# Seven-product output matmuls: in their last chunk every quarter of the output is summed in PSUM and reaches the residual once

## The chip, the core and the metric

The kernel runs on one core of a Trainium2 chip. TensorE (PE) multiplies matrices into PSUM; VectorE (DVE), ScalarE (ACT) and GpSimd (POOL) do everything elementwise; SyncE (SP) starts the DMAs. Each engine runs its own queue in order and meets the others through semaphores. The metric is the time of one execution on the device in microseconds (us), lower is better.

## The reference, cut to what matters

One decoder layer on a sequence of 1024 tokens, width 1024, in float32. Three times the running sum `h` gets a product added to it, scaled by a vector `gt`:

```
h = h + 0.5 * gt1 * (silu(a) * b) @ ffn1_w_out          # inner size 2816: stage i = 0, "FFN1"
h = h + gt2 * (mixed @ w_out)                           # inner size 1024: stage i = 1, "project_out"
h = h + 0.5 * gt3 * (silu(a) * b) @ ffn2_w_out          # inner size 2816: stage i = 2, "FFN2"
return rmsnorm(h, final_norm_w)
```

The change touches these three products and nothing else in the sources.

## The kernel before

`hT` holds `h` transposed in SBUF: eight tiles of 128 features by 1024 tokens. The output of one of the three products is seen as a 2x2 matrix of quarters, each 512 features by 512 tokens, so four tiles (`d` = 0 to 3) of 128x512. `out_seven` computes the 2x2 block product with seven block products instead of eight (the Winograd form of Strassen's scheme). The products are called `q` = 1 to 7, and with P1 to P7 for them the quarters are

```
quarter (0,0): P1 + P2                 quarter (0,1): P1 + P6 + P5 + P3
quarter (1,0): P1 + P6 + P7 + P4       quarter (1,1): P1 + P6 + P7 + P5
```

The inner dimension is cut into pairs of 128 rows; a stage runs over chunks of pairs: `CHUNKS` = (4, 3, 4) in FFN1 and FFN2, and a single chunk (4,) in project_out. Within a chunk the seven products follow each other, and a product of a chunk of 4 has four steps `k`. For a step `ops` forms the two operands (sums and differences of blocks, named s1..s4 on the weight side and t1..t4 on the other, by `left` and `right`, which are GpSimd or VectorE), and splits both into a high and a low part in a tile `wp`: two ScalarE casts (line 677) and two VectorE subtractions (line 678). A step then has 12 matmuls (line 750): four tiles `d` times three (high by high, high by low, low by high). There are four `wp` buffers here, so casts can run at most four steps, one product, ahead of the matmuls. The four 128x512 results of a product stand in PSUM, alternately in a pool named `po` and one named `s`.

`post` takes each result away. In chunks before the last, P1, P5, P6 and P7 are copied by ScalarE to SBUF accumulators `acc` (1, 5, 6, 7), from which the next chunk's PSUM tiles are seeded (line 745: a ScalarE copy into PSUM, after which the matmuls add on top); P2, P4 and P3 go straight into `hT` by `residual` (line 782: one VectorE instruction, `h + gt * x`). In the last chunk the order is 1, 5, 7, 6, 2, 4, 3. There P1, P7 and P6 are copied out and combined in `acc` by GpSimd additions (lines 715 to 727), and parts of the sums go to `hT` as they become known: P1 by one residual (from PSUM), the running sum of P1, P6 (of earlier chunks) and P7 by another (from `acc`, after line 718), P6 of the last chunk by another (from PSUM), the sums for quarters (1,1) and (0,1) by two more (from `acc`, in `second`), and P2, P4, P3 by one each (from PSUM). That is 8 residuals for each `d`, 32 in a stage. project_out has no earlier chunk, so it has no line 715, and its accumulators are parts of the large tiles `u0l` and `u0h`.

Ahead of project_out stands a merge (lines 1220 to 1234), which forms its input `mix`: per tile two DMAs from `d_gab`, matmuls into `po` (line 281), a VectorE multiplication (line 1233) and a GpSimd addition (line 1234). The squares for the norm after a stage (lines 194 to 198: ScalarE, then GpSimd or VectorE additions into `sqacc`) start in its last two products. A scheduler puts the instructions of each engine in order ahead of time, so the order of the code is not the order of the queues.

Of the kernel before, what the change touches and what calls it, by code (L numbers as in the profile page):

```python
# [9 lines left out]
F32 = mybir.dt.float32  # L10
# [7 lines left out]
P = 128  # L18
# [4 lines left out]
H2 = 512  # L23
# [29 lines left out]
class Layer:  # L53
# [541 lines left out]
    def out_seven(self, i, chunks, wsrc, gsrc, free, acc, state, then, have=None):  # L595
# [3 lines left out]
        nc = self.nc  # L599
        o, prs = 0, []  # L600
# [3 lines left out]
        chunks = prs  # L604
# [45 lines left out]
        def ops(c, k, q):  # L650
# [4 lines left out]
            left = nc.vector if len(chunks) == 1 and q in (7, 2) else nc.gpsimd  # L655
# [25 lines left out]
            if q in (2, 6) and (c, k, 8 - q) in done:  # L681
                right.tensor_sub(g("b21"), g("b21"), g("t2"))
                ren("b21", "t4")
                left.tensor_sub(g("a2"), g("a2"), g("s2"))
# [12 lines left out]

        def post(q, d, p, c, last):
            A = {x: acc[x][d] for x in acc}
            if q in (2, 3, 4):  # L700
                res(q == 4, q == 3, d, p, last)
                return
            if q == 6 and last:
                res(1, 0, d, p)
                nc.scalar.copy(A[1], p)
                return
            if q == 1 and last:
                res(0, 0, d, p)
            nc.scalar.copy(A[q], p)
            if not last:  # L710
                return
            w = A[6 if 6 in A else 1]
            if q == 1:
                if 6 in A:
                    nc.gpsimd.tensor_add(w, w, A[1])
            elif q == 7:
                nc.gpsimd.tensor_add(A[5], A[5], w)
                nc.gpsimd.tensor_add(w, w, A[7])
                nc.gpsimd.tensor_add(A[7], A[7], A[5])
                res(1, 0, d, w)  # L720

        def second(d):

            A = {x: acc[x][d] for x in acc}
            nc.gpsimd.tensor_add(A[7], A[7], A[1])
            res(1, 1, d, A[7])
            nc.gpsimd.tensor_add(A[5], A[5], A[1])
            res(0, 1, d, A[5])

        fetch()  # L730
        for c, prs in enumerate(chunks):
            last = c == len(chunks) - 1
            m = len(prs)
            for j, q in enumerate((1, 5, 7, 6, 2, 4, 3) if last else (1, 2, 5, 7, 6, 4, 3)):
                if (len(chunks) - 1 - c + j) % 2 == 0:
                    po = [self.psO.tile([P, H2], F32, name="po") for _ in range(4)]
                else:
                    po = [self.psA.tile([P, 2, H2], F32, name="s") for _ in range(2)]
                    po = [p[:, x, :] for p in po for x in range(2)]


                seeded = c > 0 and q in acc and not (last and q == 6)
                if seeded:
# [848 lines left out]
```

## Time and profile before

| | |
|---|---|
| median of 3 runs | 2452.97 us (2447.19 to 2454.83) |
| the profiled execution | 2450.27 us, its span 2448.5 us |
| busy, of the span | PE 2284.3 us, DVE 1860.7, ACT 1031.7, POOL 1252.7 |
| mean granted clock of TensorE | 0.967 of full speed |
| last chunk of FFN1, its matmuls | 650.14 to 749.85 us |
| last chunk of FFN2, its matmuls | 2329.32 to 2428.65 us |
| project_out, its matmuls | 1624.44 to 1730.8 us |

The span is the time between the first and the last instruction in the trace of one execution; the time of that execution is 1.77 us longer, and it lies 2.7 us below the median. Busy times overlap between engines. A product's four steps have 48 matmuls, and the trace lacks a few of the records.

### The profile page before, as it was taken

To read this page: it belongs to the slowest core of one execution; us is meant where nothing else is said; L and a number is where in the kernel's file an instruction comes from. 1 tells how busy PE (TensorE), PEld (TensorE's weight loads), DVE (VectorE), ACT (ScalarE), POOL (GpSimd) and SP (SyncE) were. 2 spreads that over 40 slices of the span, in tenths; PEclk is the share of its full clock that TensorE was granted. 3 is DMA by queue.
4 is the path that set the end of the run, shared out by engine and by line. 5 is a ranking of instruction groups with operands and counts; after the bars stand their busy time and mean duration, and the time that the engine had idled before them with its cause. 6 is when DMAs were issued, how large, how long until landed. Compare 5 with 4: busy or idle time off the path is not lost.

```text
span 2448.5 us, 32717 instructions
## 1 busy us (share of the span) xinstructions
PE 2284.3 (93%) x11563; PEld 1909.0 (78%) x11563; DVE 1860.7 (76%) x2790; ACT 1031.7 (42%) x1860; POOL 1252.7 (51%) x920
## 2 busy tenths in 40 slices
PE   7799999999977999999989999988889999999997
PEld 5578888878856899888868889866668888887875
DVE  8888887578999856666668887669985555558998
ACT  5333222245744422223348776624432222235655
POOL 3855454444576545555215544456754444435366
PEclk8999999999998999999998999999889999999998
DMA  9135655263204344343551221640322222255201
GB/s 345 56 112 169 201 176 186 86 232 134 78 0 136 97 142 121 110 138 110 167 165 51 74 79 57 213 153 0 103 69 78 82 78 86 85 190 186 94 1 69
DMA packets 248888, 288.32 MB, mean 118 GB/s; under 512 B 14852, under 2 KB 169236, under 8 KB 248724
## 3 DMA queue, kind: packets, MB, share of 16 engines
q1 hardware_dynamic: 248608, 286.19, 36.6%
q8 instruction: 91, 1.49, 0.3%
q14 instruction: 73, 0.60, 0.1%
q10 hardware_dynamic: 116, 0.05, 0.0%
HBM read 216.45 MB, written 69.73 MB: 117 GB/s over the span
## 4 chain that ended last, share of the span: by engine, by line
PE 31%; DVE 12%; DMA 3%; issue 2%; ACT 1%; POOL 1%; SPq 0%; DVEq 0%; ACTq 0%; POOLq 0%
PE po L281 16%; DVE wp L678 4%; PE ot L1166 2%; DVE hT L782 2%; PE po L750 2%; PE pt L1152 2%; PE s L750 2%; PE s L281 2%; PE s L1063 1%; PE s L1064 1%; DMA tn<-d_gab 1%; PE pt L855 1%; PE ot L1163 0%; PE po L495 0%; DMA hT<-d_h 0%
## 5 line engine op out<-in xcount | busy, mean ns | idle before, releaser
L750 PE MATMUL po<-wp 128*128 128x512 f32 x1176 | 293.7, 406 | 30.2 <-DVE wp L678 27.6
L281 PE MATMUL po<-u0h,wp 128*128 128x512 f32 x944 | 305.6, 395 | 9.2 <-DVE gates L991 4.9
L750 PEld LDWEIGHTS po<-wp 128*128 128x128 f32 x1176 | 227.9, 196 | 91.2 <-DVE wp L678 38.1
L281 PE MATMUL po<-u1h,wp 128*128 128x512 f32 x880 | 281.9, 391 | 3.7 <-DVE bias L544 2.2
L750 PE MATMUL s<-wp 128*128 128x512 f32 x1008 | 247.4, 403 | 21.0 <-DVE wp L678 19.7
L750 PEld LDWEIGHTS s<-wp 128*128 128x128 f32 x1008 | 195.9, 195 | 67.3 <-DVE wp L678 24.4
L334 ACT CAST wp<-S 128x1024 fp32r<-128x1024 f32 x98 | 102.9, 1050 | 302.5 <-PE po L281 300.4
L281 PEld LDWEIGHTS po<-u0h,wp 128*128 128x128 f32 x944 | 178.9, 189 | 49.9 <-DVE gates L991 5.1
L463 POOL TENSOR_TENSOR t<-t,t 128x512 f32<-128x512 f32 x38 | 55.3, 1456 | 301.8 <-DVE t L407 191.9
L281 PEld LDWEIGHTS po<-u1h,wp 128*128 128x128 f32 x880 | 165.1, 188 | 40.5 <-DVE bias L544 2.6
L281 PE MATMUL po<-u0l,wp 128*128 128x512 f32 x472 | 185.4, 393 | 0.0
L281 PE MATMUL po<-u1l,wp 128*128 128x512 f32 x440 | 172.5, 392 | 2.6 <-DVE u1l L243 2.6
L335 DVE TENSOR_TENSOR wp<-S,wp 128x1024 fp32r<-128x1024 f32 x98 | 159.8, 1630 | 15.8 <-ACT wp L334 15.6
L334 ACT CAST wp<-raw 128x1024 fp32r<-128x1024 f32 x98 | 82.0, 837 | 186.0 <-PE po L281 174.4
L341 POOL TENSOR_TENSOR S<-raw 128x512 f32<-128x512 f32 x49 | 68.7, 1403 | 157.0 <-DMA raw<-w_in 92.2
L281 PE MATMUL po<-t2h,wp 128*128 128x512 f32 x392 | 132.2, 397 | 2.2 <-ACT t2h L300 2.1
L281 PE MATMUL po<-t3h,wp 128*128 128x512 f32 x392 | 132.1, 398 | 0.2 <-DVE t L395 0.2
L281 PE MATMUL po<-t4h,wp 128*128 128x512 f32 x392 | 131.6, 396 | 0.8 <-DVE tn L399 0.7
L395 DVE TENSOR_TENSOR t<-tn,po 128x512 f32<-128x512 f32 x57 | 39.0, 685 | 110.4 <-issue 78.7
L335 DVE TENSOR_TENSOR wp<-raw,wp 128x1024 fp32r<-128x1024 f32 x98 | 113.6, 1159 | 11.9 <-ACT wp L334 11.8
L1156 DVE TENSOR_TENSOR pl<-pt,ph 128x512 fp32r<-128x512 f32 (+2 forms) x160 | 96.9, 619 | 11.9 <-ACT ph L1155 11.1
L281 PEld LDWEIGHTS po<-u0l,wp 128*128 128x128 f32 x472 | 89.7, 190 | 18.1
(471 smaller groups left out, 6248.4 us busy)
## 6 DMA issues: line engine op xcount, KB each, us to landing
raw<-ffn_w_in SPq DMA_DIRECT2D x88, 512.0 KB, 4.8
raw<-ada_w SPq DMA_DIRECT2D x56, 512.0 KB, 4.4
raw<-w_in SPq DMA_DIRECT2D x40, 512.0 KB, 4.2
d_g<-t SPq DMA_DIRECT2D x50, 256.0 KB, 2.0
d_h<-hT SPq DMA_DIRECT2D x24, 512.0 KB, 5.8
hT<-d_h SPq DMA_DIRECT2D x48, 256.0 KB, 5.3
d_g<-tg SPq DMA_DIRECT2D x38, 256.0 KB, 2.0
fw<-ada_w SPq DMA_DIRECT2D x8, 1024.0 KB, 11.1
```

Of the source, the lines that this page charges most:

```text
L281: nc.tensor.matmul(ps, a, b, start=k == 0 and q == 0, stop=k == n - 1 and q == 2)
L334: nc.scalar.copy(w[:, 0], t)
L335: nc.vector.tensor_sub(w[:, 1], t, f32(w[:, 0]))
L341: nc.gpsimd.tensor_add(s[:, 0:4], b[:, 0:4], b[:, 4:8])
L395: nc.vector.tensor_add(c, u2, p)
L463: nc.gpsimd.tensor_mul(g, g, t)
L678: nc.vector.tensor_sub(w[:, x, 1], g(n[x]), f32(w[:, x, 0]))
L750: nc.tensor.matmul(po[d], l[:, e], r, start=k == 0 and z == 0 and not seeded, stop=k == m - 1 and z == 2, skip_group_check=seeded)
L782: self.nc.vector.scalar_tensor_tensor(h, po, self.ab[:, 3 * i + 2, d:d + 1], h, op0=ALU.mult, op1=ALU.add)
L1152: nc.tensor.transpose(pt[:, o + j * P:o + (j + 1) * P], a, self.ident)
L1156: nc.vector.tensor_sub(lo, pt[:, :n], f32(hi))
L1166: nc.tensor.matmul(ot, self.V2[kt // 4][:, kt % 4, b, g, :], x[:, o:o + 2 * P], start=first and m == 0, stop=last and m == 1)
```

## The change

In the last chunk all seven products get one residual per quarter. In FFN1 and FFN2 every product of the last chunk is now seeded: P1, P5, P6, P7 from their own accumulators, P2 from accumulator 1, P4 from accumulator 7 and P3 from accumulator 6, after GpSimd has added up in them what the quarter needs (`between`). The residuals are then P2 on top of P1 for (0,0), P4 for (1,0), P3 for (0,1), all from PSUM, and one from `acc` for (1,1): 16 in a stage where there were 32. GpSimd has 16 additions of 128x512 for this where there were 24, ScalarE 28 seeds where there were 12, and 16 copies out as before. In project_out the order becomes 1, 5, 7, 2, 6, 4, 3; P1 starts in pool `s` instead of `po`; P4 is accumulated in the same PSUM tiles as P6 (`chain`), P2 and P6 are seeded from accumulator 1 and P3 from accumulator 7: 16 residuals for 32, 16 GpSimd additions for 20, 12 seeds for none, and 16 copies out as before. The number of matmuls, casts and operand sums is the same; one line of operand sums stays on VectorE in project_out as before.

```diff
@@ ops @@
-            left = nc.vector if len(chunks) == 1 and q in (7, 2) else nc.gpsimd
+            left = nc.vector if single and q == 7 else nc.gpsimd
@@
-                left.tensor_sub(g("a2"), g("a2"), g("s2"))
+                (nc.vector if single else left).tensor_sub(g("a2"), g("a2"), g("s2"))
@@ post, second -> post, between @@
-            if q == 6 and last:
-                res(1, 0, d, p)
-                nc.scalar.copy(A[1], p)
-                return
-            if q == 1 and last:
-                res(0, 0, d, p)
-            nc.scalar.copy(A[q], p)
-            if not last:
-                return
-            w = A[6 if 6 in A else 1]
-            if q == 1:
-                if 6 in A:
-                    nc.gpsimd.tensor_add(w, w, A[1])
-            elif q == 7:
-                nc.gpsimd.tensor_add(A[5], A[5], w)
-                nc.gpsimd.tensor_add(w, w, A[7])
-                nc.gpsimd.tensor_add(A[7], A[7], A[5])
-                res(1, 0, d, w)
-
-        def second(d):
-            A = {x: acc[x][d] for x in acc}
-            nc.gpsimd.tensor_add(A[7], A[7], A[1])
-            res(1, 1, d, A[7])
-            nc.gpsimd.tensor_add(A[5], A[5], A[1])
-            res(0, 1, d, A[5])
+            nc.scalar.copy(A[1 if q == 6 and single else q], p)
+            if last and q == 1 and not single:
+                nc.gpsimd.tensor_add(A[6], A[6], A[1])
+
+        def between(q):
+            for d in range(4):
+                A = {x: acc[x][d] for x in acc}
+                if single:
+                    if q == 2:
+                        nc.gpsimd.tensor_add(A[1], A[1], A[7])
+                        nc.gpsimd.tensor_sub(A[7], A[5], A[7])
+                    elif q == 6:
+                        nc.gpsimd.tensor_add(A[5], A[5], A[1])
+                        res(1, 1, d, A[5])
+                        nc.gpsimd.tensor_add(A[7], A[7], A[1])
+                elif q == 6:
+                    nc.gpsimd.tensor_add(A[7], A[7], A[6])
+                elif q == 4:
+                    nc.gpsimd.tensor_add(A[6], A[6], A[5])
+                    nc.gpsimd.tensor_add(A[7], A[7], A[5])
+                    res(1, 1, d, A[7])
@@ the loop over chunks and products @@
-            for j, q in enumerate((1, 5, 7, 6, 2, 4, 3) if last else (1, 2, 5, 7, 6, 4, 3)):
-                if (len(chunks) - 1 - c + j) % 2 == 0:
+            for j, q in enumerate((1, 2, 5, 7, 6, 4, 3) if not last else (1, 5, 7, 2, 6, 4, 3) if single else
+                                  (1, 5, 7, 6, 2, 4, 3)):
+                chain = single and q == 4
+                if not chain:
+                    if (len(chunks) - 1 - c + j + (single and q != 3)) % 2 == 0:
...
-                seeded = c > 0 and q in acc and not (last and q == 6)
-                if seeded:
+                seed = q if c > 0 and q in acc else None
+                if last:
+                    seed = {2: 1, 6: 1, 3: 7}.get(q) if single else {2: 1, 4: 7, 3: 6}.get(q, q)
+                seeded = chain or seed is not None
+                if seed is not None:
                     for d in range(4):
-                        nc.scalar.copy(po[d], acc[q][d])
+                        nc.scalar.copy(po[d], acc[seed][d])
+                if last and (q == 2 if single else q == 4):
+                    between(q)
...
                 for d in range(4):
                     post(q, d, po[d], c, last)
+                if last and q == 6:
+                    between(q)
...
-                elif last and q == 6:
-                    for d in range(4):
-                        second(d)
```

In the rows below, line numbers are those of each kernel's own file: residuals are line 782 before and 789 after, the high and low splits 677 and 678 before and 678 and 679 after, copies out 709 (and 705) before and 706 after.

VectorE in the last chunk of FFN1, around the end of product 6 (`acc_3807` and `acc_3808` are accumulators 6 and 7, `u0h`, `u1l` and `raw` hold operands, line 682 or 683 forms an operand of product 4); first before, then after:

```order
L678 TENSOR_TENSOR wp<-u0l,wp 128x512
L782 SCALAR_TENSOR_TENSOR hT<-acc_3807,ab,hT 128x512
L678 TENSOR_TENSOR wp<-u0h,wp 128x512
L782 SCALAR_TENSOR_TENSOR hT<-acc_3807,ab,hT 128x512
L678 TENSOR_TENSOR wp<-u0l,wp 128x512
L782 SCALAR_TENSOR_TENSOR hT<-acc_3807,ab,hT 128x512
L678 TENSOR_TENSOR wp<-raw,wp 128x512 x2
L682 TENSOR_TENSOR raw<-raw,u0l 128x512
L782 SCALAR_TENSOR_TENSOR hT<-acc_3807,ab,hT 128x512
L678 TENSOR_TENSOR wp<-u1h,wp 128x512
L678 TENSOR_TENSOR wp<-u0h,wp 128x512
L682 TENSOR_TENSOR u0h<-u0h,u0l 128x512
```

```order
L679 TENSOR_TENSOR wp<-u0l,wp 128x512
L679 TENSOR_TENSOR wp<-u0h,wp 128x512
L679 TENSOR_TENSOR wp<-u0l,wp 128x512
L679 TENSOR_TENSOR wp<-raw,wp 128x512 x2
L683 TENSOR_TENSOR raw<-raw,u0l 128x512
L679 TENSOR_TENSOR wp<-u1h,wp 128x512
L679 TENSOR_TENSOR wp<-u0h,wp 128x512
L683 TENSOR_TENSOR u0h<-u0h,u0l 128x512
```

The four residuals from accumulator 6, which stood between the splits of products 6 and 2, are gone, and nothing has come into their places.

VectorE a little later in the same chunk, among the splits of products 4 and 3 (`acc_3809` is accumulator 5; `s` and `po` are PSUM tiles); first before, then after:

```order
L782 SCALAR_TENSOR_TENSOR hT<-acc_3809,ab,hT 128x512
L678 TENSOR_TENSOR wp<-u1l,wp 128x512
L782 SCALAR_TENSOR_TENSOR hT<-acc_3808,ab,hT 128x512
L678 TENSOR_TENSOR wp<-raw,wp 128x512
L782 SCALAR_TENSOR_TENSOR hT<-acc_3809,ab,hT 128x512
L678 TENSOR_TENSOR wp<-raw,wp 128x512
L678 TENSOR_TENSOR wp<-u1l,wp 128x512
L678 TENSOR_TENSOR wp<-u1h,wp 128x512
L678 TENSOR_TENSOR wp<-raw,wp 128x512
L678 TENSOR_TENSOR wp<-u1h,wp 128x512 x2
L782 SCALAR_TENSOR_TENSOR hT<-s,ab,hT 128x512 x4
```

```order
L789 SCALAR_TENSOR_TENSOR hT<-acc_3808,ab,hT 128x512
L789 SCALAR_TENSOR_TENSOR hT<-po,ab,hT 128x512
L679 TENSOR_TENSOR wp<-u1l,wp 128x512
L789 SCALAR_TENSOR_TENSOR hT<-acc_3808,ab,hT 128x512
L679 TENSOR_TENSOR wp<-raw,wp 128x512
L789 SCALAR_TENSOR_TENSOR hT<-acc_3808,ab,hT 128x512
L679 TENSOR_TENSOR wp<-raw,wp 128x512
L679 TENSOR_TENSOR wp<-u1l,wp 128x512
L789 SCALAR_TENSOR_TENSOR hT<-acc_3808,ab,hT 128x512
L679 TENSOR_TENSOR wp<-u1h,wp 128x512
L679 TENSOR_TENSOR wp<-raw,wp 128x512
```

Of the residuals from `acc` those from `acc_3809` are gone; the four from `acc_3808`, which wait for GpSimd, still stand ahead of splits of product 3.

ScalarE at the start of project_out, around the copies of product 1 out of PSUM (`u0l` is the accumulator, `mix` the second operand); first before, then after:

```order
L677 CAST wp<-u1h 128x512
L677 CAST wp<-mix_14734 128x512
L709 COPY u0l<-po 128x512
L677 CAST wp<-u0h 128x512
L677 CAST wp<-mix_14734 128x512
L709 COPY u0l<-po 128x512
L677 CAST wp<-u0h 128x512
L677 CAST wp<-mix_14734 128x512
```

```order
L678 CAST wp<-u1h 128x512
L678 CAST wp<-mix_14726 128x512 x2
L678 CAST wp<-u0h 128x512 x2
L678 CAST wp<-mix_14726 128x512
L678 CAST wp<-u0h 128x512
L678 CAST wp<-mix_14726 128x512
L706 COPY u0l<-s 128x512 x4
L678 CAST wp<-u0h 128x512
```

The first copy out stood ahead of the first cast of product 5; now three steps' casts of product 5 stand ahead of the copies, and these read pool `s`.

## Rows read from the trace of the kernel before

**Rows 1.** The page: busy time of PE, and the matmuls' group with its waits.

```profile
PE 2284.3 (93%) x11563; PEld 1909.0 (78%) x11563; DVE 1860.7 (76%) x2790; ACT 1031.7 (42%) x1860; POOL 1252.7 (51%) x920
...
L750 PE MATMUL po<-wp 128*128 128x512 f32 x1176 | 293.7, 406 | 30.2 <-DVE wp L678 27.6
```

**Rows 2.** Windows of FFN1's last chunk: length, busy time per engine (x instructions), granted clock.

```profile
core 0: us, PE busy (x) PEld busy (x) DVE busy (x) ACT busy (x) POOL busy (x), PEclk, DMA share, GB/s
650.10:677.70 27.60, 25.12 (x110) 20.20 (x109) 27.60 (x32) 19.61 (x36) 21.48 (x11) 1.00 0.00 1
677.70:698.30 20.60, 20.57 (x84) 16.83 (x84) 18.47 (x17) 8.80 (x16) 13.88 (x9) 0.92 0.00 1
698.30:715.70 17.40, 13.47 (x49) 9.79 (x48) 17.33 (x18) 6.60 (x12) 14.61 (x10) 0.91 0.00 0
715.70:739.60 23.90, 16.46 (x53) 11.99 (x52) 23.90 (x23) 9.93 (x18) 16.31 (x10) 0.79 0.00 1
739.60:749.90 10.30, 10.30 (x48) 8.51 (x46) 9.74 (x17) 4.06 (x7) 0.00 (x0) 0.99 0.52 205
```

**Rows 3.** Waits of PE, 650 to 750 us: total us, times, longest.

```profile
PE s L750 <- DVE wp L678: 7.1, 2, 3.7
PE po L750 <- DVE wp L678: 6.4, 4, 2.5
PE po L750 <- ACT wp L677: 0.4, 1, 0.4
```

**Rows 4.** Timeline of PE in FFN1's last chunk: start, length, [idle before].

```profile
650.14 9.23 PE L750 MATMUL po<-wp 128*128 128x512 f32 x40
...
677.73 9.85 PE L750 MATMUL po<-wp 128*128 128x512 f32 x35 [2.51 <-DVE wp L678]
...
739.65 10.20 PE L750 MATMUL po<-wp 128*128 128x512 f32 x44
```

**Rows 5.** Timeline of DVE in the same chunk: start, length, [idle before].

```profile
680.96 1.88 DVE L678 TENSOR_TENSOR wp<-u1l,wp 128x512 fp32r<-128x512 f32 x3
...
688.07 1.77 DVE L782 SCALAR_TENSOR_TENSOR hT<-acc,ab,hT 128x512 f32<-128x512 f32 x1 [1.18 <-POOL acc L718]
689.77 1.78 DVE L678 TENSOR_TENSOR wp<-u0h,wp 128x512 fp32r<-128x512 f32 x1
...
711.45 1.40 DVE L782 SCALAR_TENSOR_TENSOR hT<-s,ab,hT 128x512 f32<-128x512 f32 x2
...
744.70 1.28 DVE L678 TENSOR_TENSOR wp<-raw,wp 128x512 fp32r<-128x512 f32 x2
```

**Rows 6.** Timeline of POOL in the same chunk: start, length, [idle before].

```profile
656.22 6.50 POOL L667 TENSOR_TENSOR u1l<-u1l,u0l 128x512 f32<-128x512 f32 x1 [24.15 <-DVE wp L678]
...
686.71 4.29 POOL L718 TENSOR_TENSOR acc<-acc,acc 128x512 f32<-128x512 f32 x3 [6.22 <-ACT acc L709]
...
710.93 1.74 POOL L684 TENSOR_TENSOR raw<-raw,u0h 128x512 f32<-128x512 f32 x1
712.64 1.28 POOL L725 TENSOR_TENSOR acc<-acc,acc 128x512 f32<-128x512 f32 x1
```

**Rows 7.** Residuals, 661 to 750 us, by source: ns min/median/max, first and last start.

```profile
L782 DVE SCALAR_TENSOR_TENSOR hT<-acc,ab,hT x12: 731/1752/1776, 688.1 to 735.1; 128x512 f32<-128x512 f32 x12
L782 DVE SCALAR_TENSOR_TENSOR hT<-po,ab,hT x11: 731/737/751, 661.5 to 749.9; 128x512 f32<-128x512 f32 x11
```

**Rows 8.** ScalarE's seeds, 640 to 750 us: ns min/median/max, first and last start.

```profile
L745 ACT COPY po<-acc x8: 577/592/610, 640.9 to 668.2; 128x512 f32<-128x512 f32 x8
```

**Rows 9.** Windows of project_out, the first stretch and the sum of six.

```profile
1624.40:1643.40 19.00, 13.78 (x48) 9.77 (x48) 18.41 (x19) 2.80 (x6) 13.06 (x8) 0.91 0.23 74
...
sum 106.40, PE 89.12 PEld 68.16 DVE 105.00 ACT 47.02 POOL 69.46; mean PE 14.85 PEld 11.36 DVE 17.50 ACT 7.84 POOL 11.58
```

**Rows 10.** Timelines of ACT, DVE and PE at the end of project_out's product 1.

```profile
1641.74 0.59 ACT L709 COPY u0l<-po 128x512 f32<-128x512 f32 x1 [16.20 <-DVE hT L782]
...
1640.96 1.40 DVE L782 SCALAR_TENSOR_TENSOR hT<-po,ab,hT 128x512 f32<-128x512 f32 x2
...
1643.41 3.82 PE L750 MATMUL s<-wp 128*128 128x512 f32 x14 [1.23 <-ACT wp L677]
```

**Rows 11.** Windows of FFN2's last chunk: the sum of five stretches.

```profile
sum 99.40, PE 86.51 PEld 67.13 DVE 97.02 ACT 50.83 POOL 75.78; mean PE 17.30 PEld 13.43 DVE 19.40 ACT 10.17 POOL 15.16
```

More of the change, by code (lines that the diff above doesn't have):

```diff
@@ L599, in out_seven @@
         nc = self.nc
+        single = len(chunks) == 1
         o, prs = 0, []
@@ L733, in out_seven @@
             m = len(prs)
-            for j, q in enumerate((1, 5, 7, 6, 2, 4, 3) if last else (1, 2, 5, 7, 6, 4, 3)):
-                if (len(chunks) - 1 - c + j) % 2 == 0:
[L736 to L739, printed above, removed]
-                seeded = c > 0 and q in acc and not (last and q == 6)
-                if seeded:
+            for j, q in enumerate((1, 2, 5, 7, 6, 4, 3) if not last else (1, 5, 7, 2, 6, 4, 3) if single else
[3 more added lines that the diff above has]
+                    if (len(chunks) - 1 - c + j + (single and q != 3)) % 2 == 0:
+                        po = [self.psO.tile([P, H2], F32, name="po") for _ in range(4)]
+                    else:
+                        po = [self.psA.tile([P, 2, H2], F32, name="s") for _ in range(2)]
+                        po = [p[:, x, :] for p in po for x in range(2)]
+                seed = q if c > 0 and q in acc else None
[3 more added lines that the diff above has]
+                if seed is not None:
                     for d in range(4):
-                        nc.scalar.copy(po[d], acc[q][d])
+                        nc.scalar.copy(po[d], acc[seed][d])
+                if last and (q == 2 if single else q == 4):
+                    between(q)
                 def mm(d, k, s, t):
```

## The prediction

> **What bounds the kernel now.** The page comes first [rows 1]: TensorE is busy for 93% of the span, so a cut on another engine pays only where TensorE waits for it. The group of output matmuls names such waits: 30.2 us of idle time, 27.6 of it ended by VectorE's low split, line 678. The windows show where [rows 2]. In FFN1's last chunk, 99.8 us long, PE is busy 85.92 us by the sum of the five rows, and VectorE is busy throughout three of them (27.60 of 27.60, 17.33 of 17.40, 23.90 of 23.90). The waits of PE there are 13.9 us, nearly all for line 678 [rows 3]. The granted clock falls to 0.79 where PE waits most [rows 2], which stretches matmuls on top of the waits. At the first stretch's pace, 40 matmuls in 9.23 us or 0.23 each [rows 4], the 336 matmuls would need 77 us. So 23 us of the 99.8 is lost, and VectorE is the lane that decides.
>
> What fills VectorE is not only its own work. Three splits in a row take 1.88 us when GpSimd idles, 0.60 from start to start; beside GpSimd's additions of `acc` (686.71 to 691.0) one takes 1.78, and the next starts 1.70 after the last [rows 5, 6]. An addition on GpSimd, 1.28 alone, is 1.74 then [rows 6]. The two take turns: each GpSimd addition costs VectorE 1.70 - 0.60 = 1.10 us. A residual that reads PSUM does not pay this: two of them take 1.40 while GpSimd adds at 710.93, 0.66 each [rows 5, 6], and the median from `po` is 737 ns against 1752 from `acc` [rows 7].
>
> FFN2's last chunk is the same picture (PE 86.51 and VectorE 97.02 busy of 99.4) [rows 11]. In project_out VectorE is busy 105.00 of 106.4 us, PE 89.12 [rows 9]. There product 1 takes 19.0 us with PE busy 13.78, since the merge shares VectorE with it; then ScalarE stands for 16.20 us before a copy out of PSUM, which waits for the residual that starts at 1640.96, and product 5's casts are queued behind that copy, so that PE waits another 1.23 us [rows 10].
>
> **The change in the FFN stages.** Removed from VectorE per stage: 8 residuals from PSUM (8 x 0.66 = 5.3 us) and 8 from `acc` (8 x 0.60 = 4.8), and 8 GpSimd additions' shadows (8 x 1.10 = 8.8): 18.9 us. That is a ceiling, for it counts only where PE waits.
>
> The Trainium skill's page "SBUF — State Buffer", section "SBUF: two separate sides", says that the port pair shared by GpSimd and VectorE is an exclusive lock held for a whole instruction, taken by a VectorE instruction with two SBUF inputs. By that a GpSimd addition would cost VectorE its 1.28 us and eight of them 10.2 in place of 8.8. The trace agrees on who pays (two SBUF inputs do, one in PSUM does not), and its 1.10 is the price used.
>
> By stretches of FFN1's chunk: up to 677.7 PE loses only its wait of 2.51 [rows 4]; four residuals and four additions go from there, 7 us of lane, but splits can run only four steps ahead, so I take 2. From 677.7 to 698.3 PE is busy 20.57 of 20.60, nothing to win. From 698.3 (product 6's end) to the last split of product 3, which ends at 744.70 + 1.28 = 746.0 [rows 5], it is the lane that sets the pace: 47.7 us. In it stand 36 VectorE instructions on SBUF, 12 residuals from PSUM and 19 GpSimd additions (1.70 apart; 6 of them the norm's, 4 operand sums). At the prices above 36 x 0.60 + 12 x 0.66 + 19 x 1.10 = 50.4, so the measured stretch is 0.946 of the sum. After: of the 24 splits and 4 operand sums of products 2, 4 and 3, six splits and three sums (three steps of product 2) can come ahead of product 6's end, since the residuals and additions that filled VectorE there are gone; before, two splits did. The fourth step's `wp` buffer comes free only at that end. 18 splits, one sum and four residuals from `acc` remain, 23 instructions; 8 residuals from PSUM; 19 GpSimd additions (12 sums, 6 of the norm, one operand sum). That is 13.8 + 5.3 + 20.9 = 40.0, times 0.946 = 37.8. The last split ends at 696.3 + 37.8 = 734.1, PE 3.9 us later as before: 738 in place of 749.9, **12 us less**. Bounds: 2 if the second part gains nothing, 18.9 if everything counts.
>
> Added: 16 seeds by ScalarE, 16 x 0.59 [rows 8] = 9.4 us. ScalarE is busy 49 of the 99.8 us by the sum of its five rows [rows 2], so I cost them at nothing; they are hidden by ScalarE's waits for free `wp` buffers. If that cover is gone each delays the casts behind it by 0.59, four per product, 2.4 us before each of three products, 7 in all. The seeds bring a new in-order wait too: product 4's wait for GpSimd (accumulator 7 plus 6) with casts behind them, product 3's likewise. GpSimd has 8 additions fewer before that point (lines 717 to 719), so I expect its sums in time. Residuals from accumulator 7 still stand ahead of splits of product 3 and wait for GpSimd; four of 1.70 against four of 0.60 are in the sum. No DMA of the chunks changes; three places on SyncE's queue swap neighbours, outside these stages.
>
> **project_out.** Removed: 8 x 0.66 + 8 x 0.60 + 4 x 1.10 = 14.5 us of VectorE's lane, times the same 0.946 = 13.7; VectorE is full here, so I count **13**. Product 1 in pool `s` no longer needs `po`, which the merge's matmuls use, and copies no longer wait for a residual (the 16.20 us wait): PE's 1.23 goes with them, inside the 13. What is queued behind the new first copies on ScalarE is the rest of product 5's casts, of which three steps now stand ahead. The chain of product 4 on product 6's tiles needs no seed, but must wait for ScalarE's copies of product 6, four of 0.59, 2.4 us; product 4 begins right after product 6, so up to 2.4 us on the path, and nothing if the matmuls of a tile start once that tile is copied. Bounds: 5 (half of 14.5 counts, and the chain's 2.4 is taken off), to 29 (336 matmuls at 0.23 in place of 106.4 us). I take 13, near the removed lane time, since only 1.4 us of VectorE's lane were idle [rows 9].
>
> FFN2 as FFN1: 12. **Sum 12 + 13 + 12 = 37.** The profiled execution of 2450.27 us would be 2413; it lies 2.7 below the median of 2452.97, so for the median 2416. Elsewhere the scheduler has changed the order of some rows (attention, the projections); I take nothing for it, some us either way.
>
> **The rivals.** *Half the gain.* GpSimd's chain becomes the late one: its sums end later than VectorE's splits, the seeds of products 4 and 3 and the residuals from `acc` wait in order, and the splits behind them. Speaking for it: before, GpSimd already makes VectorE wait for an addition, 1.18 us [rows 5], and 12 sums of 1.7 (20 us) must now lie between product 6's copies and product 3's seeds. Against it: VectorE has fewer instructions to take turns with. Then an FFN stage gains 2 to 6, project_out 8: about 17, 2436.
>
> *Everything counts.* With the waits gone the granted clock stays near 1, as in the first stretch (1.00), and the removed lane time is all gained: 18.9 + 18.9 + 18 = 57, 2396. For it: the clock falls only in stretches where PE waits. Against it: in the two stretches up to 698.3 PE has 2.5 us to give.
>
> *Slower.* GpSimd can be starved by a VectorE that has no pauses: an addition took 6.50 us at 656.22 [rows 6]. Product 4's four seeds wait for four additions and hold ScalarE's casts behind them. If each took 6.50 in place of 1.70 this is 4 x 4.8 = 19 us per FFN stage against 12 gained, 7 lost in each; project_out's copies and chain the same, its 13 cancelled: 14 more than before, 2467. It decides from three starved additions per stage. Against it: VectorE can be only four steps ahead, and it must stop when ScalarE does, which frees GpSimd.
>
> *No change.* The waits move elsewhere: the merge's DMAs, or the norm after each stage, end last in any case. Against it: VectorE's residuals and splits run to the end of the chunk (the last row of [rows 2]), and the norm begins with their results, so an earlier end moves what follows. The time would be 2446 to 2460.
>
> **How the numbers follow.** My forecast (gain of 25 to 55) 0.60, half the gain (8 to 25) 0.20, everything 0.08, no change 0.06, slower 0.06. About 0.3%, 7.4 us, is what a measurement of this kernel can tell from no change. Faster is thus 0.88, same 0.06, slower 0.06. The likeliest has 2398 to 2428 by itself. The range leaves out most of "everything", the last two cases and the smallest gains: 2398 to 2439.
>
> **What would show it.** In the profile after: 16 residuals in each stage's last chunk; the last chunk of FFN1 some 88 us long, with PE's waits for the low split from 13.9 us down to about 5, and a granted clock above 0.9 where it was 0.79; VectorE still busy at 95% or more behind product 6, so that the lane still sets the pace; splits beside GpSimd still at 1.7; seeds that wait for ScalarE's turn but not long for GpSimd. In project_out matmuls of product 1 among the merge's, and no 16 us wait before a copy. Wrong would be: waits of PE for ScalarE's casts or seeds of several us each; GpSimd additions of 4 us and more; residuals from `acc` with long waits for GpSimd and product 3's splits behind them; or the time gained in the three stages lost in the attention.

## The result, and the profile after

The changed kernel takes 2419.75 us (median of 4 runs, 2416.41 to 2422.48) beside 2452.04 of the kernel before on the same chips: ratio 0.9871, 95% interval 0.9857 to 0.9886, so 28 to 35 us less. The profiled execution has a span of 2414.6 us, 33.9 less than before.

Where these 33.9 us came from, by landmarks on TensorE in the two traces:

| stretch | before, us | after, us | difference |
|---|---|---|---|
| start to FFN1's last chunk | 650.14 | 651.42 | +1.3 |
| FFN1's last chunk, to the norm's first matmul | 99.55 | 86.96 | -12.6 |
| from there to the first projection matmul | 8.64 | 9.16 | +0.5 |
| to the merge's last matmul | 865.64 | 865.77 | +0.1 |
| project_out, to the norm's first matmul | 107.86 | 93.57 | -14.3 |
| to FFN2's first matmul | 10.30 | 12.24 | +1.9 |
| to FFN2's last chunk | 587.19 | 587.29 | +0.1 |
| FFN2's last chunk, to the norm's first matmul | 99.55 | 87.02 | -12.5 |
| to the end of the span | 19.63 | 21.17 | +1.5 |

The three stages gained 39.4 us. The first line lies before any changed code (the kernels of this study reach that chunk at 650.1 to 653.8 us), and the stretches after the stages, which hold the norms, gave 3.9 back.

The page of the changed kernel, the rows that answer to [rows 1]:

```profile
PE 2268.8 (94%) x11563; PEld 1903.5 (79%) x11563; DVE 1814.4 (75%) x2742; ACT 1055.3 (44%) x1904; POOL 1220.1 (51%) x900
...
L758 PE MATMUL po<-wp 128*128 128x512 f32 x1128 | 271.8, 397 | 17.1 <-DVE wp L679 16.3
```

PE is busy 15.5 us less, though it does the same 11563 matmuls: more of them ran at a clock granted in full (its mean over the execution rose from 0.967 to 0.973). The idle time before the output matmuls in `po` fell from 30.2 to 17.1 us.

Windows of FFN1's last chunk after, the columns of [rows 2]; the stretches are products 1, 5 and the start of 7; the rest of 7 and 6; 2; 4 in two parts; 3:

```profile
651.40:676.50 25.10, 24.89 (x110) 20.27 (x108) 24.58 (x28) 19.70 (x37) 18.40 (x8) 1.00 0.00 1
676.50:695.50 19.00, 18.98 (x84) 15.72 (x85) 14.07 (x20) 13.63 (x26) 3.29 (x3) 1.00 0.00 1
695.50:706.30 10.80, 10.80 (x49) 8.97 (x48) 10.73 (x8) 7.39 (x14) 10.80 (x7) 1.00 0.00 0
706.30:716.20 9.90, 9.41 (x39) 6.79 (x38) 9.90 (x9) 4.96 (x10) 9.90 (x7) 1.00 0.00 0
716.20:725.40 9.20, 4.46 (x12) 3.47 (x11) 9.20 (x7) 6.31 (x12) 9.20 (x7) 0.70 0.01 2
725.40:738.40 13.00, 12.32 (x50) 9.07 (x49) 12.69 (x17) 5.10 (x9) 3.18 (x3) 0.95 0.41 162
```

Read the VectorE column (the third busy time). Before product 6's end it now has slack, 4.93 us of 19.00; from there on it is as full as before, and up to 725.4 us GpSimd is busy all through beside it. PE is fed up to the last step of product 4, then starves once, and only from there is the clock low: 0.70 in that row (0.50, the lower of TensorE's two levels, 1.2 of 2.4 GHz, in the 4.5 us behind the wait, 720.9 to 725.4) and 0.95 in the last.

Waits of PE in the same chunk after, beside 7.1 and 6.4 us in [rows 3]:

```profile
PE s L758 <- DVE wp L679: 5.1, 2, 4.7
...
PE po L758 <- DVE wp L679: 0.9, 3, 0.4
```

Timeline of PE after, the starts of products 1, 7 (rest), 6, 2, 4, 4 (last step) and the norm; then before, the starts of products 7, 6, 2 and 4:

```profile
651.42 9.23 PE L758 MATMUL po<-wp 128*128 128x512 f32 x40
...
676.51 8.23 PE L758 MATMUL po<-wp 128*128 128x512 f32 x35 [0.23 <-DVE wp L679]
684.58 11.04 PE L758 MATMUL s<-wp 128*128 128x512 f32 x48
695.46 11.04 PE L758 MATMUL po<-wp 128*128 128x512 f32 x48
706.34 6.24 PE L758 MATMUL s<-wp 128*128 128x512 f32 x25
...
720.94 4.63 PE L758 MATMUL s<-wp 128*128 128x512 f32 x10 [4.74 <-DVE wp L679]
...
738.38 0.95 PE L207 MATMUL s<-ones,sqacc 128*128 128x1 f32 x8
```

```profile
672.12 3.10 PE L750 MATMUL po<-wp 128*128 128x512 f32 x12
...
687.42 11.04 PE L750 MATMUL s<-wp 128*128 128x512 f32 x48
698.30 0.39 PE L750 MATMUL po<-wp 128*128 128x512 f32 x1
...
715.75 0.44 PE L750 MATMUL s<-wp 128*128 128x512 f32 x1
```

Product 7 took 15.3 us before (672.12 to 687.42) and takes 11.4 (673.18 to 684.58); product 2 took 17.45 and takes 10.88 (695.46 to 706.34); products 4 and 3 together 33.9 and 32.0. So two products were freed, and the pair at the end hardly gained.

VectorE after, three moments: a split that waits for ScalarE's cast, a residual from `acc` beside GpSimd, and the last splits:

```profile
686.74 0.69 DVE L679 TENSOR_TENSOR wp<-u0h,wp 128x512 fp32r<-128x512 f32 x1 [2.66 <-ACT wp L678]
...
717.47 1.75 DVE L789 SCALAR_TENSOR_TENSOR hT<-acc,ab,hT 128x512 f32<-128x512 f32 x1
...
733.71 1.28 DVE L679 TENSOR_TENSOR wp<-raw,wp 128x512 fp32r<-128x512 f32 x2
```

ScalarE after, the first and the last of product 4's four seeds, with what they waited for:

```profile
698.80 0.59 ACT L751 COPY s<-acc 128x512 f32<-128x512 f32 x1 [1.03 <-POOL acc L723]
...
703.90 0.59 ACT L751 COPY s<-acc 128x512 f32<-128x512 f32 x1 [1.10 <-POOL acc L723]
```

Project_out and FFN2 after, the sums of windows that answer to [rows 9] (from 1613.5 us, four stretches) and [rows 11] (from 2306.4 us, six stretches):

```profile
sum 93.50, PE 80.50 PEld 62.14 DVE 90.07 ACT 53.23 POOL 58.58; mean PE 20.13 PEld 15.53 DVE 22.52 ACT 13.31 POOL 14.64
...
sum 86.60, PE 80.74 PEld 64.60 DVE 80.87 ACT 59.22 POOL 64.20; mean PE 13.46 PEld 10.77 DVE 13.48 ACT 9.87 POOL 10.70
```

VectorE gives up 14.9 us in project_out and 16.2 in FFN2, PE 8.6 and 5.8, and the stretches shrink by 12.9 and 12.8.

### The profile page after: what moved, and what is told of

It is laid out like the page before. It is cut to its first block, busy times and chain, and to the rows that moved or that the text cites. A ratio compares the mean times of both kernels' runs of the same rounds, so it can differ in the third digit from the quotient of the medians.

```text
span 2414.6 us, 32683 instructions
## 1 busy us (share of the span) xinstructions
PE 2268.8 (94%) x11563; PEld 1903.5 (79%) x11563; DVE 1814.4 (75%) x2742; ACT 1055.3 (44%) x1904; POOL 1220.1 (51%) x900
## 4 chain that ended last, share of the span: by engine, by line
PE 32%; DVE 9%; DMA 3%; ACT 3%; issue 2%; POOL 1%; SPq 0%; DVEq 0%; ACTq 0%; POOLq 0%
PE po L281 17%; DVE wp L679 3%; PE s L758 3%; PE po L758 3%; PE ot L1173 2%; PE pt L1159 2%; PE s L281 2%; PE s L1071 1%; DMA tn<-d_gab 1%; DVE hT L789 1%; PE s L1070 1%; DMA hT<-d_h 1%; PE pt L862 1%; PE ot L1170 0%; PE po L495 0%
## 5 line engine op out<-in xcount | busy, mean ns | idle before, releaser
L758 PE MATMUL po<-wp 128*128 128x512 f32 x1128 | 271.8, 397 | 17.1 <-DVE wp L679 16.3
L758 PEld LDWEIGHTS po<-wp 128*128 128x128 f32 x1128 | 214.6, 192 | 70.5 <-DVE wp L679 24.7
L758 PE MATMUL s<-wp 128*128 128x512 f32 x1056 | 252.5, 395 | 15.6 <-DVE wp L679 15.0
L281 PEld LDWEIGHTS po<-u1h,wp 128*128 128x128 f32 x880 | 165.1, 188 | 40.3 <-DVE bias L544 2.6
```

The source lines that it names most:

```text
L281: nc.tensor.matmul(ps, a, b, start=k == 0 and q == 0, stop=k == n - 1 and q == 2)
L758: nc.tensor.matmul(po[d], l[:, e], r, start=k == 0 and z == 0 and not seeded, stop=k == m - 1 and z == 2, skip_group_check=seeded)
```

## The experiments

The theory on trial is the lane theory: VectorE sets the pace, and each instruction or each GpSimd addition taken out of its full stretches is gained at its price. Its rivals: ScalarE's copies, which queued behind residuals; the overlap of project_out's first product with the merge; latency of a chain. Each time is a median beside the kernel before on the same chip; a ratio times 2452 us gives the differences. With intervals of some 0.0014 to either side of a ratio, the difference between two runs is known to about 5 us (an estimate from these intervals); where that is too coarse, the traces are compared by the landmarks of the table above.

### Does each half add up?

`ffn_only` has the diff in FFN1 and FFN2 and the former code in project_out; `po_only` the reverse:

```diff
 ffn_only:
-                chain = single and q == 4
+                chain = False
...
-                    seed = {2: 1, 6: 1, 3: 7}.get(q) if single else {2: 1, 4: 7, 3: 6}.get(q, q)
+                    seed = None if single else {2: 1, 4: 7, 3: 6}.get(q, q)
...
 po_only:
...
-                    seed = {2: 1, 6: 1, 3: 7}.get(q) if single else {2: 1, 4: 7, 3: 6}.get(q, q)
+                    seed = {2: 1, 6: 1, 3: 7}.get(q) if single else q if q in (1, 5, 7) else None
```

> The change in FFN1 and FFN2 alone; project_out as before. Lane theory: the stages add up, 10.8 + 11 us of the 34 measured in the traces come from the FFN stages, so 22 less than before, about 2430. Rival (the project_out part gives it, or the scheduler elsewhere): clearly other than 22, near 2440 or near 2420.

> The change in project_out alone; both FFN stages as before. Lane theory: 12 less than before, about 2440, and with the FFN part alone it adds up to the whole. Rival: what project_out gains is given back by the next stage, 2450.

`ffn_only` took 2428.86 us, ratio 0.9909 (0.9895 to 0.9923), 22.3 less; `po_only` 2437.31, 0.9948 (0.9935 to 0.9962), 12.7 less. Together 35, against 31.6 (28 to 35) for the whole: within the intervals they add up, and neither is seen to give back what the other gains.

### Residuals alone

The kernel before, without 16 residuals in each FFN stage:

```diff
-            if q == 1 and last:
+            if q == 1 and last and 6 not in A:
                 res(0, 0, d, p)
...
-            res(0, 1, d, A[5])
+            if 6 not in A:
+                res(0, 1, d, A[5])
```

(and the same for the two residuals for quarter (1,0)).

> The kernel before with 16 of the 32 residuals of each FFN stage left out (those of products 1 and 6, of the running sum and of quarter (0,1); the output lacks these parts), GpSimd's 24 additions kept. Lane theory: 8 x 0.66 + 8 x 0.60 = 10.1 of the 18.9 us of lane per stage go, pro rata 6 to 7 us per stage, 13 in all, about 2439. Rival (ScalarE's copies wait behind residuals, and the casts behind the copies; the lane does not matter): the whole FFN gain of 22, about 2430. Second rival (GpSimd's additions are all of it): nothing.

2440.0 us, ratio 0.996 (0.9947 to 0.9973): 9.8 less (6.6 to 13.0), where 13 was expected; in its trace the two chunks are 6.5 and 5.5 us shorter, where 6 to 7 was expected of each. That is nearly half of what the FFN stages gain in all. The rival that puts all on ScalarE's copies falls here, since these wait for none of the dropped residuals any more, and so does the one that puts all on GpSimd. The rest, 22.3 - 9.8 = 12.5, is left for what else the change does there: eight GpSimd additions fewer per stage, the seeds, and the places of both.

### ScalarE's copies set free

```diff
             if q == 6 and last:
-                res(1, 0, d, p)
+                if 6 not in A:
+                    res(1, 0, d, p)
                 nc.scalar.copy(A[1], p)
+                if 6 in A:
+                    res(1, 0, d, A[1])
                 return
```

(and likewise for product 1.)

> The kernel before, in the FFN stages the residuals of products 1 and 6 of the last chunk read the copy in the accumulator instead of PSUM, so ScalarE's copy waits for no residual. Same number of instructions on VectorE. Lane theory: no gain, and up to 8 x 1.04 us per stage dearer where GpSimd adds beside them: 2450 to 2460. Rival (ScalarE's copies waiting behind residuals are the cause): most of the FFN gain, 2430 to 2437.

2460.41 us, ratio 1.0036 (1.0022 to 1.0050): 8.8 slower. ScalarE's copies of product 6, the first of them in the kernel before, where it waited 7.5 us for a residual, then all four in this kernel:

```profile
707.13 0.59 ACT L705 COPY acc<-s 128x512 f32<-128x512 f32 x1 [7.50 <-DVE hT L782]
```

```profile
701.17 1.07 ACT L706 COPY acc<-s 128x512 f32<-128x512 f32 x2 [0.61 <-PE s L755]
702.54 1.07 ACT L706 COPY acc<-s 128x512 f32<-128x512 f32 x2 [0.29 <-PE s L755]
```

PE in product 2 soon after, and three of the residuals that VectorE does while PE waits there:

```profile
722.97 4.63 PE L755 MATMUL po<-wp 128*128 128x512 f32 x10 [8.46 <-DVE wp L678]
...
714.49 5.09 DVE L787 SCALAR_TENSOR_TENSOR hT<-acc,ab,hT 128x512 f32<-128x512 f32 x3
```

The copies and the casts behind them come at once, and PE waits longer than before, for VectorE. The run changes two things, so it gives no price for either: it shows that a wait of ScalarE of 7.5 us was worth less than what residuals lose by reading SBUF beside GpSimd (1.70 us each in the row above, 0.66 from PSUM; eight per stage, so at most 8.3 us, and 4.4 is what the run lost). `no_extra_residuals` frees the same copies and does not gain more than the lane theory gives.

### The price of a GpSimd addition

```diff
                 elif q == 4:
+                    nc.gpsimd.tensor_add(A[1], A[1], A[5])
+                    nc.gpsimd.tensor_add(A[1], A[1], A[5])
                     nc.gpsimd.tensor_add(A[6], A[6], A[5])
```

> The changed kernel with 8 more GpSimd additions in the last chunk of each FFN stage, before product 4's (into accumulator 1, which nothing reads any more). Lane theory: each costs VectorE 1.10 us, 8 x 1.10 x 0.946 = 8.3 us per stage, 16.6 in all: about 2436. With a lock that holds VectorE for a whole addition of 1.28 us: 9.7 per stage, 2439. Rival (GpSimd's additions are hidden, only the residuals count): 2420.

2429.5 us, ratio 0.9911 (0.9895 to 0.9927): 9.8 more than the changed kernel, 4.9 per stage where 8.3 was expected. The price per addition is not what failed; the place is. In this kernel: GpSimd, the first six of the eight added instructions in FFN1; the window of products 7 and 6; PE in product 2; VectorE's last splits:

```profile
683.88 2.54 POOL L725 TENSOR_TENSOR acc<-acc,acc 128x512 f32<-128x512 f32 x2 [8.91 <-ACT po L753]
686.38 3.46 POOL L726 TENSOR_TENSOR acc<-acc,acc 128x512 f32<-128x512 f32 x2
689.79 3.43 POOL L725 TENSOR_TENSOR acc<-acc,acc 128x512 f32<-128x512 f32 x2
```

```profile
675.60:694.50 18.90, 18.90 (x83) 15.66 (x84) 14.77 (x16) 13.59 (x26) 10.62 (x7) 1.00 0.00 1
```

```profile
701.25 3.02 PE L760 MATMUL po<-wp 128*128 128x512 f32 x12 [0.89 <-DVE wp L679]
706.32 2.79 PE L760 MATMUL po<-wp 128*128 128x512 f32 x11 [2.05 <-DVE wp L679]
...
738.69 1.28 DVE L679 TENSOR_TENSOR wp<-raw,wp 128x512 fp32r<-128x512 f32 x2
```

They wait for nothing of product 6, so the scheduler put six of the eight ahead of its end, where VectorE has its slack: GpSimd is busy 10.62 us there instead of 3.29, and PE stays at 18.90 of 18.90. But the six are not free. VectorE does 16 instructions in that stretch where it did 20, and product 2, which waited for nothing in the changed kernel, waits 0.89 and 2.05 us. From product 6's end at 694.5 to the last split's end at 740.0 there stand 28 VectorE instructions on SBUF, 8 from PSUM and 23 additions. At the prediction's prices this is 16.8 + 5.3 + 25.3 = 47.4 us, and the stretch took 45.4; in the changed kernel the same sum is 41.7 and the stretch 39.5. The sum grew by 5.7 and the stretch by 5.9, so the prices hold, and of the 8.8 us that eight additions cost, 3.1 went into slack.

### Sums moved to VectorE, and residuals moved forward

`sums_on_vector` has the FFN stages' three additions of `between` on VectorE, `early_residual` spares one of them:

```diff
 sums_on_vector:
-                    nc.gpsimd.tensor_add(A[7], A[7], A[6])
+                    nc.vector.tensor_add(A[7], A[7], A[6])
                 elif q == 4:
-                    nc.gpsimd.tensor_add(A[6], A[6], A[5])
-                    nc.gpsimd.tensor_add(A[7], A[7], A[5])
+                    nc.vector.tensor_add(A[6], A[6], A[5])
+                    nc.vector.tensor_add(A[7], A[7], A[5])
 early_residual:
+            if last and q == 5 and not single:
+                res(1, 1, d, A[5])
...
                 elif q == 6:
                     nc.gpsimd.tensor_add(A[7], A[7], A[6])
+                    nc.gpsimd.tensor_add(A[6], A[6], A[5])
                 elif q == 4:
-                    nc.gpsimd.tensor_add(A[6], A[6], A[5])
-                    nc.gpsimd.tensor_add(A[7], A[7], A[5])
                     res(1, 1, d, A[7])
```

and `early_and_vector` is `early_residual` with its two remaining sums on VectorE.

> The changed kernel with the 12 sums after product 6 of each FFN stage (accumulators 6 and 7) on VectorE instead of GpSimd. Lane theory: 0.60 us each instead of 1.10, 12 x 0.50 x 0.946 = 5.7 us less per stage, 2408. Rival (VectorE's order: the sums wait for ScalarE's copies of product 6 and hold splits behind them): as much lost as won, 2420, or slower. Second rival (GpSimd's additions are hidden): 12 x 0.60 more per stage, 2434.

> The changed kernel in which quarter (1,1) gets two residuals in the FFN stages, accumulator 5 after product 5 and accumulator 7 after product 6, so that four GpSimd additions go, and accumulator 6's sums are placed ahead of product 2 in the code. Lane theory: the four additions go from the last stretch, 4 x 1.10 x 0.946 = 4.2 us per stage, the four more residuals lie where VectorE has slack: 2411. Rival: VectorE's four more residuals cost as much as the additions, 2420.

> The early-residual kernel with its eight remaining sums behind product 6 of each FFN stage on VectorE. Lane theory: 8 x 0.50 x 0.946 = 3.8 us per stage less than that kernel's 2410: 2402. Rival (the lane is no longer the bound there, a latency is: sums, seeds, casts in a chain): 2410.

2411.12 us (0.9834, 0.9819 to 0.9848), 2409.95 (0.9832, 0.9816 to 0.9848) and 2403.4 (0.9809, 0.9796 to 0.9822): against the changed kernel 9, 10 and 15 us less, where 12, 9 and 18 were expected. In the traces the two FFN chunks together are 7.7, 4.7 and 10.6 us shorter, and the lane's prices gave 11.4, 8.4 and 16: some 55 to 70% of it, and that `early_residual` came out as said by its median is in part luck. The four residuals of `early_residual` on VectorE:

```profile
677.67 2.73 DVE L790 SCALAR_TENSOR_TENSOR hT<-acc,ab,hT 128x512 f32<-128x512 f32 x4
```

They lie in the slack, at 0.66 us each, since GpSimd idles. In `early_and_vector`, waits of PE and the windows of FFN1's last chunk from product 2 on (700 to 735 us):

```profile
PE po L759 <- DVE wp L679: 1.7, 4, 0.6
PE s L759 <- DVE wp L679: 1.6, 1, 1.6
```

```profile
700.00:711.00 11.00, 9.37 (x42) 7.39 (x41) 11.00 (x17) 6.09 (x11) 2.22 (x1) 1.00 0.00 0
711.00:722.00 11.00, 10.47 (x47) 8.33 (x46) 11.00 (x10) 9.46 (x18) 9.21 (x6) 1.00 0.00 1
722.00:735.00 13.00, 10.19 (x46) 7.74 (x45) 12.19 (x19) 5.52 (x10) 3.06 (x3) 1.00 0.61 223
```

More work on the full engine made it faster: an addition takes VectorE 0.60 us of its own, and 1.10 when GpSimd does it beside a full VectorE. PE's waits are down to 3.3 us, none long, and the clock is granted in full throughout this chunk; in FFN2's, where one wait of 2.5 us is left, a window of 12 us behind it has 0.86. This kernel is some 6 us faster than each of the other two. The chunks now last 81.1 and 82.3 us, and the prediction's 77 us for their matmuls alone are near, so less of the lane's price can be gained.

### The rest of GpSimd's additions

`norm_adds_vector` puts the squares' additions of line 198 on VectorE in all stages, `po_sums_vector` project_out's four kinds of sums:

```diff
 norm_adds_vector:
-            (nc.vector if (i != 2 and d == 3 if hf else d > 3) else nc.gpsimd).tensor_add(state[hf], state[hf], q)
+            nc.vector.tensor_add(state[hf], state[hf], q)
 po_sums_vector:
                     if q == 2:
-                        nc.gpsimd.tensor_add(A[1], A[1], A[7])
-                        nc.gpsimd.tensor_sub(A[7], A[5], A[7])
+                        nc.vector.tensor_add(A[1], A[1], A[7])
+                        nc.vector.tensor_sub(A[7], A[5], A[7])
```

(and likewise for the two additions behind product 6.)

> The changed kernel with all additions of squares (line 198) on VectorE, in all three stages. Lane theory: 6 additions per stage lie beside splits in the last stretch, 6 x 0.50 x 0.946 = 2.8 us per stage, 8.5 in all: 2411. Rival (the additions come in VectorE's order behind ScalarE's squares and hold up splits, or the norm after the stage gets longer): 2420 or slower.

> The changed kernel with project_out's 16 sums on VectorE instead of GpSimd. Lane theory: 16 x 0.50 x 0.946 = 7.6 us less at most; eight of them lie where VectorE still has 1 to 2 us of slack: 2413. Rival (VectorE's order: sums wait for ScalarE's copies and hold splits back): 2420 or slower.

2413.78 us (0.9852, 0.9839 to 0.9865) and 2414.52 (0.9856, 0.9844 to 0.9869): about 5 and 4 us less than the changed kernel, half of what was expected of each, and the intervals overlap with that of the changed kernel, so the times alone show no gain. By its trace `po_sums_vector` has project_out, from the merge's last matmul to FFN2's first, in 100.3 us (1615.54 to 1715.79) where the changed kernel has 105.8 (1613.31 to 1719.12) and five other kernels with the same code there have 106.1 to 107.3. `norm_adds_vector` gained 3.1 us in FFN1's chunk, as reckoned, but 0.8 in FFN2's and nothing in project_out (106.5, from 1614.42 to 1720.96). PE there:

```profile
1681.65 11.17 PE L758 MATMUL s<-wp 128*128 128x512 f32 x48 [2.63 <-ACT u0l L706]
...
1710.46 1.36 PE L207 MATMUL s<-ones,sqacc 128*128 128x1 f32 x8 [4.14 <-DVE sqacc L198]
```

Product 4, chained on product 6's tiles, waits 2.63 us for a copy, and the norm waits 4.14 us for additions that now stand in VectorE's own queue. Work taken off the lane is not gained there; that the order of the queue takes it back is the likely reading, not a shown one.

### Project_out: pool or lane?

`po_other_bank` swaps the pools, `po_no_chain` gives product 4 its own tiles, so that the pools alternate as before the change:

```diff
 po_other_bank:
-                    if (len(chunks) - 1 - c + j + (single and q != 3)) % 2 == 0:
+                    if (len(chunks) - 1 - c + j + (single and q == 3)) % 2 == 0:
 po_no_chain:
-                chain = single and q == 4
+                chain = False
...
-                    if (len(chunks) - 1 - c + j + (single and q != 3)) % 2 == 0:
+                    if (len(chunks) - 1 - c + j) % 2 == 0:
...
-                    seed = {2: 1, 6: 1, 3: 7}.get(q) if single else {2: 1, 4: 7, 3: 6}.get(q, q)
+                    seed = {2: 1, 6: 1, 4: 1, 3: 7}.get(q) if single else {2: 1, 4: 7, 3: 6}.get(q, q)
```

> The changed kernel in which project_out's products take the other pool each (product 1 in po, which the merge's matmuls use, as before the change), all else the same. Lane theory: fewer residuals and sums make nearly all of project_out's 12.7, the pool at most the 1.2 us wait and the 11 early matmuls (2.5 us): 2420 to 2424. Rival (the gain is that product 1 overlaps the merge): 8 to 12 lost, about 2430.

2436.85 us, ratio 0.9941 (0.9929 to 0.9954): 17 more than the changed kernel, which is what the rival said, and more than project_out had gained. But the trace puts most of the loss at the other end of the stage. PE in this kernel, from product 4's end:

```profile
1687.05 12.21 PE L758 MATMUL po<-wp 128*128 128x512 f32 x41 [2.39 <-DVE wp L679]
1709.44 1.87 PE L207 MATMUL s<-ones,sqacc 128*128 128x1 f32 x8 [10.19 <-DVE sqacc L198]
1711.17 5.47 PE L758 MATMUL s<-wp 128*128 128x512 f32 x12
1716.44 1.08 PE L230 MATMUL s<-tn,ones 128*128 128x512 f32 x2
```

Product 3 now stands in pool `s`, from which the norm's tile (line 207) comes too, and behind the norm's first matmul in PE's queue; that waits 10.19 us for squares. The swap had moved two things, so the time told nothing of the first. The trace does: product 2 starts 42.2 us behind the merge's last matmul here, 40.3 in the changed kernel, and 40.6 to 41.9 in other kernels whose product 1 overlaps the merge. By this the overlap is worth about 2 us at most.

> The changed kernel in which project_out's product 4 has its own PSUM tiles, seeded from accumulator 1 (four ScalarE copies more), so that the pools alternate as before the change: product 1 in po, product 3 in po. In the run with the pools swapped product 3 stood in s, whose tiles the norm uses too, and PE waited 10.2 us there between product 4 and product 3; here it does not. Lane theory: fewer residuals and sums make most of the 12.7; against the changed kernel lost are the 2.5 us of product 1's early matmuls, 1.2 us of waiting and up to 2.4 us for seeds: 2421 to 2426. Rival (the overlap of product 1 with the merge is the gain): 2430 to 2433.

2416.98 us, ratio 0.9871 (0.9852 to 0.9890): the changed kernel's ratio to the last digit. With product 1 in `po`, behind the merge, and without the chain, no loss can be measured in the time. In the trace project_out takes 96.7 us to the norm's first matmul, 3.2 more than in the changed kernel, and 106.75 to FFN2's first, 0.9 more and inside the 105.8 to 107.3 of the kernels with the changed code. Product 4 waits 2.33 us for a seed here, where the chain waits 0.35 for a copy, so the chain is worth some 2 us. Neither the overlap with the merge nor the chain carries the gain of project_out; what this kernel shares with the changed one is the fewer residuals and sums, and the order 1, 5, 7, 2, 6. These two were not tried apart, so that the first carries it rests on the FFN stages, where the residuals were, and on `po_sums_vector`.

## Why the prediction was right, point by point

**The bound.** That VectorE's lane decides in the FFN chunks held in every experiment there that took load from it or added load to it, if often for less than its full price, and the one that freed ScalarE instead lost time. In `norm_adds_vector` it held in FFN1 alone: FFN2 gained 0.8 us and project_out nothing.

**FFN, up to 677.7 us.** 2 us were taken for a wait of 2.51; the wait fell to 0.23. **From there to product 6's end** the prediction had nothing to win, since PE was busy 20.57 of 20.60. This step failed by 1.6 us: with the wait ahead of it gone the granted clock in this stretch rose from 0.92 to 1.00, and the same 84 recorded matmuls took 18.98 us instead of 20.57. Before, the low clock lay in the first 4.3 us behind the wait (0.60 from 677.7 to 682.0, 1.00 from there on). Busy was not full pace, and the row had said so in its clock column; it also speaks against the prediction's remark that the clock falls only in stretches where PE waits.

**From product 6's end.** The trace has 24 instructions on SBUF, 8 from PSUM and 20 additions, one VectorE instruction and one addition more than were counted (14.4 + 5.3 + 22.0 = 41.7), in 39.5 us (695.5 to 733.71 + 1.28 = 735.0): 0.947 of the sum, beside 0.946 before. The lane's prices carried over. The chunk gained 12.6 us where 12 was forecast, and FFN2's 12.5, but the closeness is in part luck: up to product 6's end the gain was 4.1 instead of 2, and from there to the last split 8.2 instead of 9.9, and these two misses cancel.

**Price of an addition.** 1.10 us, from the interval of 1.70 against 0.60, reproduces the full stretch after the change and that of `double_sums`. Additions moved to VectorE gave two thirds of the difference between 1.10 and 0.60 (`sums_on_vector`), and a part of the price is not paid where VectorE has slack (`double_sums`). The Trainium skill's page "SBUF — State Buffer", section "SBUF: two separate sides", has the shared ports locked for a whole instruction, which by the trace's 1.28 us for an addition alone is the higher price. These runs do not tell the two apart, and they agree with that section that it is VectorE's instruction with two SBUF inputs that contends with GpSimd (residuals from `acc` after: 1753 ns in the median, from `po`, which is PSUM, 742).

**Added seeds.** Costed at nothing. The longest wait of product 4's seeds for GpSimd was 1.10 us, and PE waited for no seed.

**Project_out.** 13 forecast, 14.3 in the trace of the stage, 12.7 by `po_only`. The value came out, and so did the split of it: the pool and the chain were said to count for at most a few us, and count for about 2 each by the traces. Which part of the 13 is the order's is not known.

**The rest.** 37 was the sum; the stages gave 39.4 in the trace. 1.3 of jitter and the longer tails (0.5 + 1.9 + 1.5) leave 33.9, and by medians the gain is 32: 2419.75 us where 2416 was forecast. The prediction took the tails as unchanged. In project_out's tail PE waited 7.56 us ahead of the matmuls of line 230, 5.61 before; why the norms do not follow all of the earlier end was not tried.

**What was said to show.** Waits for the low split of about 5 us (6.0), VectorE at 95% or more behind product 6 (it is), seeds with short waits: right. So was project_out, where 11 matmuls of product 1 stand among the merge's and no copy waits 16 us. A clock above 0.9 where it was 0.79: wrong, for it is 0.70 in the 9.2 us in which the wait of 4.74 is left; ahead of them it is 1.00, behind them 0.95.

**The rivals.** Half the gain: no residual from `acc` waited for GpSimd in FFN1's chunk, and product 4's seeds waited 1.10 us at most. The one long wait of PE that is left, 4.74 us, falls where VectorE's splits and residuals take turns with GpSimd's additions. Everything: 39 in the stages against 56 (the prediction wrote 57; its terms add up to 55.8), since part of what VectorE was spared before product 6's end became slack (4.93 us). Starved additions: the four ahead of product 4's seeds took 1.7 us each, not 6.5.

## What to carry to other kernels

Make the sum for the stretch in which an engine is full, with what other engines cost it in that stretch, and check first that the sum reproduces the stretch before; its ratio then carried over here (0.946, 0.947, and 0.96 in `double_sums`). Recount which instructions stand in the stretch, since a change can push some across its edge. Moving elementwise work to GpSimd to relieve a full VectorE can load it more than doing it there: compare the interval of VectorE's instructions beside GpSimd with their interval alone, not the two engines' durations. And before an experiment swaps two buffers, list everything that the swap moves: here it moved product 3 into the norm's pool, and the time pointed at the wrong cause.

## What was not expected of the hardware

The same addition of 128x512 costs a full VectorE 1.10 us from GpSimd and 0.60 if VectorE does it itself, and less where VectorE has slack: eight more of them made the lane's sum 5.7 us longer instead of 8.8. The granted clock came back to 1.00 in a stretch that had 0.92 with no wait inside it, only one of 2.51 us ahead of it; with waits of at most 1.6 us in `early_and_vector` it stayed at 1.00 to the end of FFN1's last chunk.
